# Weight-sum stores seven steps behind their load, thirteen pairs, and halves every eight steps, in a one-core attention and feed-forward block

## The chip, the core and the metric

The kernel runs on one core of a Trainium2 chip. A core has a matrix engine (TensorE, PE in the profile; its weight loads are PEld), a vector engine (VectorE, DVE), a scalar engine (ScalarE, ACT), GpSimd (POOL), and a queue engine, SyncE (SP), which issues nearly all transfers of this kernel to 16 DMA engines. Each engine works through its own instructions in order and waits for semaphores of the others. The metric is the device time of one execution in microseconds, as the median of several runs.

## What is computed

One layer with 256 tokens of 2048 features, in float32: three attention branches (six "forgetting" heads, six stick-breaking heads, four heads over a memory of 256 tokens), gated and merged, then a feed-forward part with a causal convolution over three tokens.

```python
h = rms_norm(x, g_mix[l])
proj = h @ w_in[l]
fq, fk, fv, f_logit, sq, sk, sv, mq, gates = jnp.split(proj, cuts, axis=-1)
...
g = jax.nn.sigmoid(gates.reshape(b, s, N_BRANCH, D_MODEL) + b_gate[l])
merged = (g[:, :, 0] * (o_fox @ w_br_fox[l])
          + g[:, :, 1] * (o_sb @ w_br_sb[l])
          + g[:, :, 2] * (o_mem @ w_br_mem[l]))
x = x + merged @ w_out[l]
h2 = rms_norm(x, g_ffn[l])
u = causal_depthwise_conv(h2 @ w_up[l], conv_w[l], conv_b[l])
u_gate, u_val = jnp.split(u, 2, axis=-1)
x = x + (jax.nn.silu(u_gate) * u_val) @ w_down[l]
```

## The kernel before

**Products.** Every weight is split into a high and a low part on the chip, and a product is the sum of three passes (high by high, low by high, high by low). `product` (L157) walks the 2048 rows of a weight in eight pieces of 256 rows by up to 512 columns. For each, `piece` (L136) loads the raw weights through SP's queue (L141) into one of four raw buffers, casts them to the high part on ACT (L142), and subtracts to get the low part on DVE (L143); four buffers hold high and low parts. Then twelve matmuls follow (two row tiles, two token tiles, three passes), and `tick` (L103) advances the generators by one step. So one step is one piece. Since there are four raw buffers, the load of a piece waits for the subtraction of the piece four steps before it.

**Stages.** In order: the memory's keys and values, then the heads' stages `mq`, `f0` to `f4`, `s0` to `s4` (products with parts of `w_in`; `f4` has 262 columns and `s4` 256, the others 512, and all have eight steps), with the work of the heads advanced by `tick` between the pieces. Then the gates and branches in two rounds (`m` = 0 and 1): gates by `product` for the first (`g0`) and by `blocked` for the others, then per round two times eight steps of branch products (forgetting three, memory two, stick-breaking three). After them the output product `o`, the up projection with the convolution, and the down projection `d`. `blocked` (L355) computes 2 by 2 blocks either with eight products ("e" in a plan) or with seven ("s"), which needs sums of weight blocks and of activations.

**Weight sums ahead.** The plans of `o` and `d` have 8 and 25 seven-product pairs. For each, three sums of blocks of the weights (`sums_in`, L247: instructions at L249, L250, L251 on DVE) are made ahead and kept in device memory. The list `halves` (L239) has two halves per pair. `pair_sums_ahead` (L282) takes a whole pair: a load of 1 MB (L292), the sums some steps later, a store of 1 MB (L302). `half_sums` (L259) takes half a pair: two loads of 256 KB (L268), sums of half the size, and a store of 512 KB (L278) from a single staging buffer, so that its next load waits until the store has landed. They are generators in `background`, and `tick` advances them one step per piece, except inside `blocked` for the gates, where `tick(beside=False)` leaves them alone.

- Heads' stages, from `f0` on (L771): pairs with period 6, sums after 3 steps, store after 5, in two staging buffers in turn, until `s3` has been issued (L938).
- Gates and branches (L962): halves with period 6, sums after 2, store after 4, until the output product begins (L1095). These stages have 48 such steps: 16 in the first gate's products and 16 in each round of branches.
- Up projection (L1132): the remaining 17 pairs, with period 8, sums after 1, store after 5.

**Order.** A planner orders the instructions of each engine from their dependences, program order and its own reckoning of durations. `in_order` (a name for `keep_in_program_order`, L234) pins an instruction behind the instruction traced just before it on the same engine; it says nothing of what comes after. The loads and stores of the sums, and the sums, are pinned in this way. The weight loads of the products in these stages are not pinned (`pinned[0]` is false from L732 on), so that the planner may draw them forward.

**Memory shared by tag.** The staging buffers of the pairs (`staged`, L764, tag "xres") share their place with `xs` (L951), sums of x that `x_sums` (L953) writes from its fifth step on, and later with the residual (`xres_again`, loaded again at L1067 in the second round of branches).

Of the kernel before, what the change touches and what calls it, by code (L numbers as in the profile page):

```python
# [9 lines left out]
F32 = mybir.dt.float32  # L10
# [5 lines left out]
P = 128  # L16
# [21 lines left out]
PF = 6  # L38
# [4 lines left out]
def hybrid_block(  # L43
# [25 lines left out]
    nc = tc.nc  # L69
# [31 lines left out]
    background = []  # L101
# [16 lines left out]
    issued = set()  # L118
# [84 lines left out]
    def k_tiles(name):  # L203
# [30 lines left out]
    in_order = tc.keep_in_program_order  # L234
# [4 lines left out]
    halves = deque(  # L239
        (name, by_k(w), nb, pr, h)  # L240
        for name, w, plans in (("o", w_out, o_plans), ("d", w_down, d_plans))
        for nb, plan in enumerate(plans)
        for pr in range(plan.count("s"))
        for h in range(2)
    )

    def sums_in(w):  # L247
        both = w[:, 1:2].to_broadcast([P, 2, w.shape[2]])
        in_order(nc.vector.tensor_tensor(w[:, 0:2], w[:, 0:4:3], both, ALU.add))  # L249
        in_order(nc.vector.tensor_tensor(w[:, T2], w[:, T1], w[:, T2], ALU.add))  # L250
        in_order(nc.vector.tensor_tensor(w[:, T4], w[:, T2], w[:, T4], ALU.add))  # L251

    def kept_for(name, nb, pr):
        if (name, nb, pr) not in sums_of:
            at = f"kept_{name}{nb}_{pr}"
            sums_of[name, nb, pr] = dram.tile([P, 4, 512], F32, tag=at, name=at)
        return sums_of[name, nb, pr]

    def half_sums(staging, period, add, store, end):  # L259

        while halves and end not in issued:
            name, wv, nb, pr, h = halves.popleft()
            kept = kept_for(name, nb, pr)
            w = staging(f"pre_{name}{nb}_{pr}_{h}").rearrange("p (i c) -> p i c", i=4)
            n0 = nb * PIECE + h * 256
            for n in range(2):
                in_order(
                    nc.sync.dma_start(  # L268
                        w.rearrange("p (k n) c -> p k n c", k=2)[:, :, n],
                        wv[:, 2 * pr : 2 * pr + 2, n0 + n * 512 : n0 + n * 512 + 256],  # L270
                    )
                )
            for _ in range(add):
                yield
            sums_in(w)
            for _ in range(store - add):
                yield
            in_order(nc.sync.dma_start(kept[:, :, h * 256 : (h + 1) * 256], w))  # L278
            for _ in range(period - store):
                yield  # L280

    def pair_sums_ahead(staging, period, add, store, end=None, delay=0):  # L282

        for _ in range(delay):
            yield
        while len(halves) > 1 and halves[0][-1] == 0 and end not in issued:
            name, wv, nb, pr, _ = halves.popleft()
            halves.popleft()
            kept = kept_for(name, nb, pr)
            w = staging(f"pre_{name}{nb}_{pr}")  # L290
            in_order(
                nc.sync.dma_start(  # L292
                    w.rearrange("p (k c) -> p k c", k=2), wv[:, 2 * pr : 2 * pr + 2, nb * PIECE : (nb + 1) * PIECE]
                )
            )
            w = w.rearrange("p (i c) -> p i c", i=4)
            for _ in range(add):
                yield
            sums_in(w)
            for _ in range(store - add):  # L300
                yield
            in_order(nc.sync.dma_start(kept, w))  # L302
            for _ in range(period - store):
                yield

    def parts(src, name):
        n = src.shape[1]
# [287 lines left out]
    gp = mix.enter_context(tc.tile_pool(name="gp", bufs=3))  # L595

    def block(name, dt=F32):
        return bp.tile([P, 1024], dt, tag="blk", name=name)

    def heads_of(b):  # L600
        return b.rearrange("p (h s) -> p h s", h=4)

    def rows_of(b):
        return b.rearrange("p (t n) -> p t n", t=NT)
# [68 lines left out]
    w = {}  # L673
# [30 lines left out]
    for k in range(KT):  # L704
# [18 lines left out]
        for _ in range(0 if k < 3 else 1 if k < 8 else 3):  # L723
            if squares:
                j, t = squares.popleft()
# [41 lines left out]
    def in_turn(name):  # L767
        turn[0] += 1
        return staged[:, turn[0] % 2]

    background.append(pair_sums_ahead(in_turn, PF, 3, 5, "s3"))  # L771
    qm = heads_of(block("qm"))
    y = norm_heads(ps, rstd, "mq")
    later(heads_T(y, qm, (gh[:, 2:3], gh[:, 2:3]), 2, "mq"))
# [160 lines left out]
        later(sb_head(h))  # L935

    ps = proj(C_SB + 1536, 512, "s3")
    issued.add("s3")  # L938
    vs[0] = rows_of(block("vs0"))
    for t in range(NT):  # L940
        nc.scalar.activation(vs[0][:, t], ps[t], AF.Copy, scale=rstd[:, t : t + 1])
# [11 lines left out]
    def x_sums():  # L953
# [6 lines left out]

    background.append(x_sums())
    background.append(  # L962
        half_sums(lambda name: gp.tile([P, 1024], F32, tag="pre", bufs=1, name=name), 6, 2, 4, "merged")
    )


# [143 lines left out]
    for nb, plan in enumerate(o_plans):  # L1110
# [19 lines left out]
    ends_tile = lambda name, dt: ff.tile([P, 2, PIECE], dt, tag="ends", bufs=1, name=name)  # L1130
    background.append(
        pair_sums_ahead(lambda name: ends_tile(name, F32).rearrange("p i c -> p (i c)"), 8, 1, 5, delay=DU)  # L1132
    )

# [196 lines left out]
```

## Time and profile before

| | |
|---|---|
| Median of 3 runs | 1465.25 us (1464.0 to 1466.06) |
| The profiled execution: its time, and its span | 1466.82 us, 1465.1 us |
| DMA, mean over the span | 260 GB/s, 381.08 MB |
| Pair loads and stores in the heads' stages | 12 and 12, 1 MB each |
| Half stores in gates and branches | 8, 512 KB each |
| Pair loads and stores in the up projection | 17 and 17, 1 MB each |

The span runs from the first to the last instruction that was profiled; the run's own time has a little more around it. A row of a timeline gives start and duration in microseconds, the engine (SPq is SP's queue), the line of the kernel, what is written from what, and in brackets how long the engine had been idle and what ended that. Rows of TensorE overlap, because matmuls are pipelined and their ends are modelled: the distance from start to start is what counts. A row of the view of a tile gives the line, the count, and shortest, median and longest duration in nanoseconds.

### The profile page before, as it was taken

The page shows a single profiled execution, that of the slowest core. Times are in us where ns is not written, and L with a number is a line of the kernel's source. Part 1 is how long each engine was busy: PE and PEld are TensorE (multiplying, and loading weights), DVE is VectorE, ACT ScalarE, POOL GpSimd, SP SyncE. Part 2 cuts the span into 40 slices and gives each one's busy share as a digit, 9 for nine tenths or more (in the row PEclk, how much of TensorE's full clock was granted, in tenths as well). Part 3 has the DMA queues.
Part 4 walks back from the last instruction along what each step waited for, and adds up shares of the span by engine and source line. Part 5 has one row for each costly group of instructions (what it writes and reads, how often), then busy time and mean ns, then how long its engine had stood idle before and what let it go on. Part 6 is the DMA issues. An engine that isn't in the chain of part 4 may idle for free.

```text
span 1465.1 us, 20555 instructions
## 1 busy us (share of the span) xinstructions
PE 1457.1 (99%) x7314; PEld 1231.1 (84%) x7314; DVE 1214.0 (83%) x1794; ACT 848.9 (58%) x1212; POOL 17.0 (1%) x48
## 2 busy tenths in 40 slices
PE   9999999999999999999999999999999999999998
PEld 7888888888888888878888888888888888888887
DVE  5778767776898899987987888888888877999878
ACT  6755445564654555545666656556556566676664
POOL 0000000110000000000000000000000000000000
PEclk9999999999999999999999999999999999999999
DMA  8697798677669676788878888888888866889995
GB/s 299 201 328 251 265 335 294 210 230 211 215 203 284 193 228 198 257 269 265 269 218 231 273 276 300 276 283 291 282 282 293 273 202 203 251 289 323 309 327 216
DMA packets 164262, 381.08 MB, mean 260 GB/s; under 512 B 12298, under 2 KB 29598, under 8 KB 160190
## 3 DMA queue, kind: packets, MB, share of 16 engines
q1 hardware_dynamic: 162750, 377.52, 78.9%
q10 hardware_dynamic: 1328, 2.11, 0.4%
q8 instruction: 57, 0.93, 0.3%
q14 instruction: 47, 0.39, 0.1%
q0 software_dynamic: 80, 0.13, 0.0%
HBM read 343.01 MB, written 36.70 MB: 259 GB/s over the span
## 4 chain that ended last, share of the span: by engine, by line
PE 95%; DVE 2%; DMA 2%; issue 1%; ACT 0%; SPq 0%; DVEq 0%; ACTq 0%
PE u L1220 22%; PE u L1221 11%; PE xg L318 4%; PE xg L317 4%; PE xg L316 4%; PE xd L317 3%; PE xd L316 3%; PE xd L318 3%; PE f L316 2%; PE f L317 2%; PE f L318 2%; PE s L318 2%; PE s L316 2%; PE s L317 2%; PE yd L317 2%; PE yd L316 2%
## 5 line engine op out<-in xcount | busy, mean ns | idle before, releaser
L1220 PE MATMUL u<-hT,hi_u 128*128 128x512 f32 x1232 | 428.3, 394 | 0.0
L1221 PE MATMUL u<-hT,lo_u 128*128 128x256 f32 x1232 | 341.3, 277 | 0.0
L1220 PEld LDWEIGHTS u<-hT,hi_u 128*128 128x128 f32 x1232 | 231.0, 188 | 53.6
L143 DVE TENSOR_TENSOR lo_u<-raw_u,hi_u 128x1024 fp32r<-128x1024 f32 x176 | 215.3, 1224 | 73.2 <-ACT hi_u L142 72.7
L142 ACT CAST hi_u<-raw_u 128x1024 fp32r<-128x1024 f32 x176 | 184.7, 1050 | 136.7 <-PE u L1220 106.4
L1221 PEld LDWEIGHTS u<-hT,lo_u 128*128 128x128 f32 x1232 | 231.3, 188 | 0.0
L311 DVE TENSOR_TENSOR lo_d<-raw_d,hi_d 128x1024 fp32r<-128x1024 f32 x88 | 106.7, 1222 | 17.2 <-ACT hi_d L310 14.9
L310 ACT CAST hi_d<-raw_d 128x1024 fp32r<-128x1024 f32 x88 | 91.7, 1053 | 39.4 <-PE xd L317 11.6
L310 ACT CAST hi_g<-raw_g 128x1024 fp32r<-128x1024 f32 (+1 forms) x80 | 77.1, 972 | 48.9 <-PE xg L317 18.6
L311 DVE TENSOR_TENSOR lo_g<-raw_g,hi_g 128x1024 fp32r<-128x1024 f32 (+1 forms) x80 | 88.7, 1120 | 4.2 <-ACT hi_g L310 4.1
L142 ACT CAST hi_f<-raw_f 128x1024 fp32r<-128x1024 f32 (+1 forms) x40 | 38.6, 967 | 51.6 <-PE f L317 46.3
L316 PE MATMUL xg<-hi_g,xT 128*128 128x512 f32 x175 | 68.1, 389 | 0.0
L318 PE MATMUL xg<-lo_g,xT 128*128 128x512 f32 x175 | 68.1, 389 | 0.0
L317 PE MATMUL xg<-hi_g,xT 128*128 128x512 f32 x175 | 68.1, 389 | 0.0
L143 DVE TENSOR_TENSOR lo_f<-raw_f,hi_f 128x1024 fp32r<-128x1024 f32 (+1 forms) x40 | 44.6, 1118 | 21.9 <-ACT hi_f L142 21.2
L1220 PE MATMUL u<-hT_rest,hi_u 128*128 128x512 f32 x176 | 62.0, 394 | 0.0
L142 ACT CAST hi_b<-raw_b 128x1024 fp32r<-128x1024 f32 x32 | 33.5, 1051 | 47.7 <-DMA raw_b<-in_w_br_fox_dram 13.5
L143 DVE TENSOR_TENSOR lo_s<-raw_s,hi_s 128x1024 fp32r<-128x1024 f32 (+1 forms) x40 | 44.5, 1114 | 19.9 <-ACT hi_s L142 19.5
L142 ACT CAST hi_s<-raw_s 128x1024 fp32r<-128x1024 f32 (+1 forms) x40 | 38.2, 961 | 36.9 <-PE s L317 21.5
L1171 ACT ACTIVATE y<-u,taps 128x256 f32<-128x256 f32 x88 | 49.6, 596 | 15.6 <-DVE u L1166 15.5
L318 PE MATMUL xd<-lo_d,aT 128*128 128x512 f32 x148 | 57.6, 389 | 0.0
L316 PE MATMUL xd<-hi_d,aT 128*128 128x512 f32 x148 | 57.6, 389 | 0.0
(520 smaller groups left out, 3475.9 us busy)
## 6 DMA issues: line engine op xcount, KB each, us to landing
raw_u<-in_w_up_dram SPq DMA_DIRECT2D x176, 512.0 KB, 4.8
raw_g<-in_w_in_dram SPq DMA_DIRECT2D x96, 512.0 KB, 4.5
raw_d<-in_w_down_dram SPq DMA_DIRECT2D x63, 512.0 KB, 5.6
pre_d<-in_w_down_dram SPq DMA_DIRECT2D x17, 1024.0 KB, 7.3
kept_d<-pre_d SPq DMA_DIRECT2D x17, 1024.0 KB, 6.2
raw_f<-in_w_in_dram SPq DMA_DIRECT2D x32, 512.0 KB, 4.7
raw_s<-in_w_in_dram SPq DMA_DIRECT2D x32, 512.0 KB, 4.9
raw_t_d<-kept_d SPq DMA_DIRECT2D x25, 512.0 KB, 6.1
```

What stands on the lines that cost most here:

```text
L142: pin(nc.scalar.copy(hi[:, :m], raw[:, :m]))
L143: pin(nc.vector.tensor_tensor(lo[:, :m], raw[:, :m], hi[:, :m].bitcast(F32), ALU.subtract))
L310: nc.scalar.copy(hi[:, :n], src)
L311: nc.vector.tensor_tensor(lo[:, :n], src, hi[:, :n].bitcast(F32), ALU.subtract)
L316: fix(nc.tensor.matmul(o, lhsT=ah, rhs=w[0], start=first, stop=False))
L317: fix(nc.tensor.matmul(o, lhsT=al, rhs=w[0], start=False, stop=False))
L318: fix(nc.tensor.matmul(o, lhsT=ah, rhs=w[1], start=False, stop=last))
L1171: nc.scalar.activation(y, u[:, 2:], AF.Identity, scale=tap(2), bias=tap(3))
L1220: nc.tensor.matmul(ps[i], lhsT=hi[:, j, c], rhs=hT(k + j), start=first, stop=False)
L1221: nc.tensor.matmul(ps[i][:, :S], lhsT=lo[:, j, c], rhs=hT(k + j)[:, :S], start=False, stop=last)
```

## The change

In the heads' stages the store of a pair is made seven steps after its load in place of five, which is one step after the next pair's load. To allow this, the generator keeps the stores that are due in a list with the step at which each is to go. The generator ends after thirteen pairs, not when `s3` has been issued: the thirteenth pair is loaded in the first step of `s4` and stored in its last. In gates and branches a half takes eight steps, not six, and its store goes after five, not four, so that six halves are made there in place of eight. The up projection's 17 pairs keep their steps.

```diff
-    def pair_sums_ahead(staging, period, add, store, end=None, delay=0):
-
+    def pair_sums_ahead(staging, period, add, store, most=99, delay=0):
+
+        due = deque()
+        clock = 0
         for _ in range(delay):
             yield
-        while len(halves) > 1 and halves[0][-1] == 0 and end not in issued:
+
+        def step():
+            while due and due[0][0] <= clock:
+                _, kept, w = due.popleft()
+                in_order(nc.sync.dma_start(kept, w))
+
+        while len(halves) > 1 and halves[0][-1] == 0 and most:
+            most -= 1
             name, wv, nb, pr, _ = halves.popleft()
             halves.popleft()
             kept = kept_for(name, nb, pr)
...
             w = w.rearrange("p (i c) -> p i c", i=4)
-            for _ in range(add):
+            due.append((clock + store, kept, w))
+            for t in range(period):
+                if t == add:
+                    sums_in(w)
+                step()
+                clock += 1
                 yield
-            sums_in(w)
-            for _ in range(store - add):
-                yield
-            in_order(nc.sync.dma_start(kept, w))
-            for _ in range(period - store):
-                yield
+        while due:
+            step()
+            clock += 1
+            yield
...
-    background.append(pair_sums_ahead(in_turn, PF, 3, 5, "s3"))
+    background.append(pair_sums_ahead(in_turn, PF, 3, 7, most=13))
...
-    issued.add("s3")
...
-        half_sums(lambda name: gp.tile([P, 1024], F32, tag="pre", bufs=1, name=name), 6, 2, 4, "merged")
+        half_sums(lambda name: gp.tile([P, 1024], F32, tag="pre", bufs=1, name=name), 8, 2, 5, "merged")
```

## Prediction

> **What bounds the kernel now.** I read the first two parts of the page first.
>
> ```profile
> span 1465.1 us, 20555 instructions
> PE 1457.1 (99%) x7314; PEld 1231.1 (84%) x7314; DVE 1214.0 (83%) x1794; ACT 848.9 (58%) x1212; POOL 17.0 (1%) x48
> ```
>
> TensorE is busy for all but 8.0 us (1465.1 - 1457.1). The change touches no matmul, so it can win only moments in which a matmul starts late. I therefore went through TensorE's timeline start by start. In a 512-column product the starts are 0.23 us apart (the first two rows below); what exceeds that is lost. Outside the start-up there are three losses near 1 us, one in the heads' stages and two in the second round of branches:
>
> ```profile
> 201.60 0.39 PE L317 MATMUL s<-hi_s,xT 128*128 128x512 f32 x1
> 201.83 0.39 PE L318 MATMUL s<-lo_s,xT 128*128 128x512 f32 x1
> 202.33 0.50 PE L316 MATMUL s<-hi_s,xT 128*128 128x512 f32 x1
> 202.67 0.40 PE L317 MATMUL s<-hi_s,xT 128*128 128x512 f32 x1
> 203.59 0.50 PE L318 MATMUL s<-lo_s,xT 128*128 128x512 f32 x1 [0.53 <-DVE lo_s L143]
> 203.93 0.40 PE L316 MATMUL s<-hi_s,xT 128*128 128x512 f32 x1
> ...
> 636.59 0.39 PE L317 MATMUL b<-hi_b,oT 128*128 128x512 f32 x1
> 637.70 0.50 PE L318 MATMUL b<-lo_b,oT 128*128 128x512 f32 x1 [0.72 <-DVE lo_b L143]
> ...
> 660.35 0.39 PE L317 MATMUL b<-hi_b,oT 128*128 128x512 f32 x1
> 661.48 0.50 PE L318 MATMUL b<-lo_b,oT 128*128 128x512 f32 x1 [0.74 <-DVE lo_b L143]
> ```
>
> - At 201.8: steps of 0.50, 0.34, 0.92 and 0.34 in place of 0.23 each, so 0.27 + 0.11 + 0.69 + 0.11 = **1.18 us**.
> - At 636.6: 1.11, so 0.88, and the stretched step behind it, taken from the first group, 0.11: **0.99 us**.
> - At 660.4: 1.13, so 0.90 + 0.11 = **1.01 us**.
>
> Together 3.18 us, 0.22% of the time. That is about all the change can win; what remains is whether it wins it, and what it makes late elsewhere.
>
> **Part 1: the store goes seven steps behind its load.** The chain of waits around 201 says what was late:
>
> ```profile
> 192.38 0.69 DVE staged L251
> ...
> 193.52 7.68 DMA raw_s<-in_w_in_dram
> ...
> 201.23 1.06 ACT hi_s L142
> ```
>
> The last of the sums (L251) ends at 193.07. The store (L302 in the next group) waited for it and is issued at 193.09; only then comes the weight load behind it on SP's queue, at 193.52, which takes 7.68 us. Its cast and subtraction come too late for TensorE. That load's buffer had been free since 189.5, when the subtraction four pieces back (the four raw buffers) ended, and the sums come directly behind that subtraction:
>
> ```profile
> 188.76 0.70 DVE L143 TENSOR_TENSOR lo_f<-raw_f,hi_f 128x524 fp32r<-128x524 f32 x1 [0.76 <-ACT hi_f L142]
> ```
>
> and on SP's queue:
>
> ```profile
> 193.09 0.34 SPq L302 DMA_DIRECT2D kept_o<-staged  x1
> ...
> 205.41 0.42 SPq L292 DMA_DIRECT2D staged<-in_w_down_dram  x1
> 206.23 0.37 SPq L141 DMA_DIRECT2D raw_s<-in_w_in_dram  x1
> 210.93 0.34 SPq L302 DMA_DIRECT2D kept_o<-staged  x1
> ```
>
> So the weight load lost 193.52 - 189.5 = 4.0 us behind a store that could not go yet. With the store written two ticks later it is pinned behind the weight piece of that tick, so this load must go ahead of it. It then lands 4.0 us earlier, at about 197.2; cast (1.06) and subtraction (1.24) end by 199.6, ahead of the 202.3 at which TensorE wants it. The next load stays behind the store, but is wanted one piece (12 x 0.23 = 2.7 us) later. Gain: 1.18 us. The other stores gain nothing: there the planner already issues the next pair's load and a weight piece ahead of the store, as the rows at 205 to 211 show (load, weight piece, store), because the store is pinned only behind what was traced before it and the later load is not pinned behind the store. The staging buffer that the store holds longer is reused 12 ticks after its load, so five ticks (five pieces, 13 us) remain for a landing of 6.6 us (quoted below): no wait.
>
> **Part 2: the thirteenth pair.** Its load, three sums and store now fall into the narrow stage of 256 columns, where a piece lasts half as long. The sums, from the views of the two staging tiles:
>
> ```profile
> L249 DVE TENSOR_TENSOR staged<-staged x12: 1205/1218/1221, 84.9 to 281.3; 128x1024 f32<-128x1024 f32 x12
> DMA to landing us min/median/max: 4.2/6.6/7.7
> ```
>
> ```profile
> L249 DVE TENSOR_TENSOR pre_d<-pre_d x8: 684/685/685, 314.9 to 648.0; 128x512 f32<-128x512 f32 x8
> L251 DVE TENSOR_TENSOR pre_d<-pre_d x8: 418/423/425, 317.1 to 652.7; 128x256 f32<-128x256 f32 x8
> ```
>
> A pair costs DVE 1.22 + 2 x 0.69 = 2.60 us (L251 from the chain above; L250 is as large), a half 0.685 + 2 x 0.42 = 1.53 us. In all, DVE trades two halves (3.06) for a pair (2.60): 0.46 us less, of no worth by itself under a full TensorE. The bytes are the same. What counts is where they fall (timelines of ACT, DVE and TensorE, then the page's list of DMA issues):
>
> ```profile
> 301.51 0.61 ACT L142 CAST hi_s<-raw_s 128x512 fp32r<-128x512 f32 x1
> ```
>
> ```profile
> 304.96 0.69 DVE L143 TENSOR_TENSOR lo_s<-raw_s,hi_s 128x512 fp32r<-128x512 f32 x1 [1.10 <-ACT hi_s L142]
> 307.22 1.29 DVE L143 TENSOR_TENSOR lo_s<-raw_s,hi_s 128x512 fp32r<-128x512 f32 x2 [1.10 <-ACT hi_s L142]
> 309.59 1.23 DVE L143 TENSOR_TENSOR lo_g<-raw_g,hi_g 128x1024 fp32r<-128x1024 f32 x1 [1.07 <-PE s L317]
> ```
>
> ```profile
> 306.91 0.28 PE L318 MATMUL s<-lo_s,xT 128*128 128x256 f32 x1
> 312.90 0.39 PE L318 MATMUL g<-lo_g,xT 128*128 128x512 f32 x1
> ```
>
> ```profile
> raw_s<-in_w_in_dram SPq DMA_DIRECT2D x32, 512.0 KB, 4.9
> ```
>
> DVE idles 1.10 + 1.10 + 1.07 = 3.27 us in these few steps, which covers the 2.60 us of sums; without that cover they would stand in front of the stage's last subtractions. The store is pinned behind the stage's last weight piece, and the first gate piece competes with it. A weight load just behind such a store took 7.68 us against a median of 4.9, so 2.8 us more. The first gate piece is split by 310.82 (309.59 + 1.23) and wanted at 312.90: 2.08 us of slack. Store ahead of it on the queue: 2.8 - 2.08 = 0.7 us late, plus 0.1 of stretched pitch, 0.8. Store behind it: 0. Below nothing is excluded, since nothing is late in that stage now. If sums and store both delayed it and the idle time covered nothing, 2.60 + 2.8 - 2.08 = 3.3 us, the outer end. The quoted queue rows have the store now before, now after the weight piece whose buffer comes free just after the sums, so I take the middle of 0 and 0.8: **0.4 us lost**.
>
> How fast that queue drains decides the 0.7:
>
> ```profile
> 193.00:202.00 9.00, 9.00 (x45) 7.43 (x43) 2.86 (x6) 3.20 (x7) 0.00 (x0) 1.00 1.03 398
> ```
>
> (Last columns: DMA busy share and GB/s.) With the DMA engines full, at 193 to 202, 398 GB/s went through. The Trainium skill (DMA: Bandwidth & Descriptors, section Where 436 GB/s comes from) puts the limit between HBM and SBUF at about 358 GB/s per core; the row is above it, and the measurement decides. By the page a 1.05 MB store would hold the queue 2.9 us, by the row 2.6 us; the sum would be 0.3 us worse by the page.
>
> **Part 3: gates and branches, eight ticks per half.** Only the first gate projections and the two rounds of branches advance this generator, 16 ticks each. Period 6 starts eight halves in 48 ticks and lets one straddle from the first round into the second; period 8 starts six, two per stretch. In the second round that means two sets of sums and two stores in place of three. And a second wait shrinks. There is one staging buffer, so a load waits for the store before it to land (SP's waits from 430 to 670, total, times and longest; then SP's timeline):
>
> ```profile
> SPq L268 <- DMA kept_d<-pre_d: 11.9, 5, 4.7
> ```
>
> ```profile
> 615.18 0.53 SPq L278 DMA_DIRECT2D kept_d<-pre_d  x1
> 615.76 0.62 SPq L1067 DMA_DIRECT2D xres_again<-in_x_dram  x1
> 621.13 0.88 SPq L268 DMA_DIRECT2D pre_d<-in_w_down_dram  x2
> 622.11 1.44 SPq L141 DMA_DIRECT2D raw_b<-in_w_br_sb_dram  x3
> 636.20 0.52 SPq L278 DMA_DIRECT2D kept_d<-pre_d  x1
> 640.34 0.88 SPq L268 DMA_DIRECT2D pre_d<-in_w_down_dram  x2
> ```
>
> The next branch's weights (L141, 622.11) stand behind such a load, which stood behind the store: 5.9 us from store to load here, 4.1 us at 636.20 to 640.34, then 512 KB more on the full queue. Now the second round's loads come behind its first and ninth piece, early in each half, not ahead of the stick-breaking branch's weights. The stall at 636.6 loses one set of sums (1.53 us, more than its 0.99) from DVE's queue ahead of the late subtraction, and that at 660.4 loses another and the load at 640.34. The set that stays falls behind the third piece of each half, where nothing is late now. Gain: 2.00 us if both go, 0 if neither. I take both: 2.00.
>
> **The sum.** 1.18 + 2.00 - 0.4 = 2.78 us. The profiled execution took 1466.82 us around its span of 1465.1; the sum makes that 1464.04. The median of the runs shown is 1.57 lower, 1465.25, and becomes **1462.5**.
>
> **Rivals.**
> - *The x loads make the branch stalls.* The two 1 MB reloads of x (the row at 615.76 is one) fall into the same 25 us; if they alone make the weights late, sums and stores matter little. For it: the weights behind them were late by DMA. Against: the stall at 660 comes some 40 us after that row. Then 1465.25 - 1.18 + 0.4 = 1464.5.
> - *The change does not do what it says in the heads' stages*: the planner had most stores there already, and reorders around the one that counts so that another weight piece is late. Then 1465.25 - 2.00 + 0.4 = 1463.7.
> - *Slower: ACT waits for the thirteenth store.* The weight sums of x (xs, cast at L332) take the staging buffers' memory, so their first cast waits until the last store has landed. The planner draws them forward into the narrow stage:
>
> ```profile
> 293.27 0.61 ACT L332 CAST xs<-xr 128x512 fp32r<-128x512 f32 x1
> ```
>
>   Now the last store cannot be issued before about 304.1: its sums, 2.60 us, stand behind the fourth subtraction of the narrow stage, which I put beside the fifth cast at 301.51. It lands 6.6 us later at 310.7, and the xs cast ends at 311.3. Casts of weight pieces queued behind it on ACT wait too: for the fifth piece (now cast at 301.51), cast 0.61 and subtraction 0.69 would end at 312.6, wanted at 306.9: 5.7 us, so 1465.25 - 3.18 + 5.7 = 1467.8. It decides for slower where the cast stands ahead of the sixth piece or an earlier one: a piece lasts about 1.4 us there (four lie between the rows at 306.91 and 312.90), so the sixth costs 4.3, above the 3.18 won. Against: if the planner reckons with the later store, it places the cast later, and it is needed only in the gate stages.
>
> **How the numbers follow.** Forecast 0.50, x loads 0.17, heads unchanged 0.15, ACT's wait 0.13, anything else 0.05. Differences within 0.2% (2.9 us) cannot be told from none. The forecast's own range, residue 0 to 0.8 and the runs' scatter of 1 us, is 1461.3 to 1463.5; about half of it lies below 1462.3, and with what I may have missed (smaller late starts elsewhere) faster gets 0.34. The x loads, unchanged heads and the rest of the forecast are "same": 0.56. ACT's wait from its dearer places makes slower 0.10. The range reaches from 1461.3 to 1466.5, up to but not over the dear end of the slower rival.
>
> **What would show it.** Right: no late start of TensorE near 201, 636 and 660; near 190 a weight load ahead of the store that went at 193.09; SP's waits at L268 for kept_d well under 11.9 us; at most 0.8 us lost where the gates begin. Wrong: late starts in the last 256-column stage, ACT idle ahead of the xs cast, or branch subtractions as late as now with fewer sums ahead of them.

## The result and the profile after

| | before | changed |
|---|---|---|
| Median of 14 runs | 1464.72 us | 1462.28 us |
| Ratio, with its 95% interval | | 0.9982 [0.9974, 0.9991] |
| Profiled execution, its span | 1465.1 us | 1459.8 us |

The change makes the kernel 2.44 us faster; 1462.5 us was forecast, 2.75 below the 1465.25 shown then. The first lines of the changed kernel's page:

```profile
span 1459.8 us, 20547 instructions
PE 1454.0 (100%) x7314; PEld 1230.1 (84%) x7314; DVE 1213.4 (83%) x1791; ACT 850.0 (58%) x1212; POOL 19.3 (1%) x48
```

The idle time of TensorE went from 8.0 to 5.8 us (1459.8 - 1454.0). The two spans differ by more than the medians. Part of it lies ahead of `f0` in code that the change doesn't reach (the first matmul of s0 starts 1.54 us earlier, in the rows below). So I compare stretches between matmuls. TensorE's timeline, before and then after: the first matmul of s0, of the gates, of the first branches and of the output product.

```profile
193.86 0.40 PE L316 MATMUL s<-hi_s,xT 128*128 128x512 f32 x1
...
312.43 0.40 PE L316 MATMUL g<-hi_g,xT 128*128 128x512 f32 x1
...
446.78 0.39 PE L316 MATMUL b<-hi_b,oT 128*128 128x512 f32 x1
...
663.89 0.39 PE L316 MATMUL xo<-hi_o,mT 128*128 128x512 f32 x1
```

```profile
192.32 0.40 PE L328 MATMUL s<-hi_s,xT 128*128 128x512 f32 x1
...
309.68 0.40 PE L328 MATMUL g<-hi_g,xT 128*128 128x512 f32 x1
...
444.39 0.39 PE L328 MATMUL b<-hi_b,oT 128*128 128x512 f32 x1
...
658.84 0.39 PE L328 MATMUL xo<-hi_o,mT 128*128 128x512 f32 x1
```

From s0 to the gates it is 118.57 before and 117.36 after (1.21 won), through the first round's gates 134.35 and 134.71 (0.36 lost), from there to the output product 217.11 and 214.45 (2.66 won). From there to the last matmul both take 796.7. The place of the late start near 200 is now regular, 0.23 from start to start:

```profile
200.74 0.39 PE L329 MATMUL s<-hi_s,xT 128*128 128x512 f32 x1
200.97 0.39 PE L330 MATMUL s<-lo_s,xT 128*128 128x512 f32 x1
201.20 0.39 PE L328 MATMUL s<-hi_s,xT 128*128 128x512 f32 x1
```

SP's queue shows why. One weight load now stands between the pair's load and the store, and the store still waits for its sums, with one weight load fewer behind it:

```profile
186.95 0.42 SPq L301 DMA_DIRECT2D staged<-in_w_out_dram  x1
188.06 0.37 SPq L141 DMA_DIRECT2D raw_s<-in_w_in_dram  x1
191.66 0.34 SPq L292 DMA_DIRECT2D kept_o<-staged  x1
192.09 10.48 SPq L141 DMA_DIRECT2D raw_s<-in_w_in_dram  x5
```

Over both rounds a load of a half (L268) still waits for the store before it, but once, not five times (SP's waits from 430 to 670: total, times, longest). In the second round SP issues the loads of two halves and two stores, in place of two and three:

```profile
SPq L268 <- DMA kept_d<-pre_d: 3.6, 1, 3.6
```

```profile
602.62 0.97 SPq L268 DMA_DIRECT2D pre_d<-in_w_down_dram  x2
...
619.32 0.53 SPq L278 DMA_DIRECT2D kept_d<-pre_d  x1
...
623.65 0.97 SPq L268 DMA_DIRECT2D pre_d<-in_w_down_dram  x2
...
641.09 0.53 SPq L278 DMA_DIRECT2D kept_d<-pre_d  x1
```

The one late start over 0.2 us left after `f0` is not in the profile of before. It lies in the gates, where no background step runs; here are TensorE's timeline and then DVE's:

```profile
421.76 0.39 PE L329 MATMUL xg<-hi_t_g,xT 128*128 128x512 f32 x1
422.28 0.50 PE L330 MATMUL xg<-lo_t_g,xT 128*128 128x512 f32 x1
422.62 0.40 PE L328 MATMUL yg<-hi_t_g,xs 128*128 128x512 f32 x1
```

```profile
420.39 0.69 DVE L440 TENSOR_TENSOR t_g<-raw_g 128x512 f32<-128x512 f32 x1 [1.69 <-DMA raw_g<-in_w_in_dram]
421.00 1.22 DVE L323 TENSOR_TENSOR lo_t_g<-t_g,hi_t_g 128x1024 fp32r<-128x1024 f32 x1
```

DVE waits 1.69 us for a weight transfer that an addition of the next pair needs (L440), and the subtraction that TensorE needs (L323) stands behind it: 0.29 + 0.11 = 0.40 us.

### The profile page after: what moved, and what is told of

Its sections match the earlier page's. It is cut to its first block, busy times and chain, and to the rows that moved or that the text cites. A ratio compares the mean times of both kernels' runs of the same rounds, so it can differ in the third digit from the quotient of the medians.

```text
span 1459.8 us, 20547 instructions
## 1 busy us (share of the span) xinstructions
PE 1454.0 (100%) x7314; PEld 1230.1 (84%) x7314; DVE 1213.4 (83%) x1791; ACT 850.0 (58%) x1212; POOL 19.3 (1%) x48
## 4 chain that ended last, share of the span: by engine, by line
PE 97%; DVE 1%; DMA 1%; issue 0%; SPq 0%; ACT 0%; DVEq 0%; ACTq 0%
PE u L1231 22%; PE u L1232 11%; PE xd L329 3%; PE xd L330 3%; PE xd L328 3%; PE xg L330 3%; PE xg L329 3%; PE xg L328 3%; PE s L328 2%; PE s L330 2%; PE f L330 2%; PE f L328 2%; PE f L329 2%; PE s L329 2%; PE b L330 2%; PE b L328 2%
## 5 line engine op out<-in xcount | busy, mean ns | idle before, releaser
L323 DVE TENSOR_TENSOR lo_d<-raw_d,hi_d 128x1024 fp32r<-128x1024 f32 x88 | 106.7, 1222 | 16.2 <-ACT hi_d L322 13.8
L323 DVE TENSOR_TENSOR lo_g<-raw_g,hi_g 128x1024 fp32r<-128x1024 f32 (+1 forms) x80 | 88.6, 1119 | 4.1 <-ACT hi_g L322 4.1
```

Of the source, the lines that this page charges most:

```text
L323: nc.vector.tensor_tensor(lo[:, :n], src, hi[:, :n].bitcast(F32), ALU.subtract)
```

## The experiments

Each run has a profile, and all are read in the same way: the three stretches as above, and the late starts over 0.2 us with the stretched step behind each. Times are in us; the ratio is to the kernel before on the same chip.

| kernel | s0 to gates | first gates | to the output product | late starts (place: size) | median | ratio |
|---|---|---|---|---|---|---|
| before | 118.57 | 134.35 | 217.11 | 202: 1.2, 594: 0.5, 637: 1.0, 660: 1.0 | 1464.72 | |
| before, again | 118.19 | 134.42 | 216.38 | 201: 0.8, 628: 1.0, 635: 1.0 | 1464.1 (one run) | |
| changed | 117.36 | 134.71 | 214.45 | 422: 0.4 | 1462.28 | 0.9982 [0.9974, 0.9991] |
| changed, again | 117.35 | 134.62 | 214.92 | 422: 0.3, 592: 0.6 | 1461.94 | 0.9984 [0.9974, 0.9993] |
| lag only | 117.35 | 134.83 | 217.13 | 382: 0.5, 630: 0.8, 636: 0.9, 660: 0.9 | 1463.46 | 0.9995 [0.9986, 1.0004] |
| halves only | 117.92 | 134.69 | 214.31 | 201: 0.5, 381: 0.4 | 1462.85 | 0.9989 [0.9981, 0.9998] |
| store after five | 118.37 | 134.68 | 214.77 | 201: 0.9, 381: 0.2 | 1462.68 | 0.9988 [0.9979, 0.9997] |
| halves of six | 117.35 | 134.87 | 216.15 | 381: 0.6, 629: 0.7, 635: 0.9 | 1463.54 | 0.9994 [0.9985, 1.0003] |
| twelve pairs | 117.35 | 134.25 | 214.54 | none | 1462.64 | 0.9989 [0.9979, 1.0] |
| halves four later | 117.35 | 134.27 | 216.58 | 594: 0.3, 622: 0.2, 659: 1.3 | 1463.46 | 0.9995 [0.9982, 1.0007] |
| x later (on before) | 117.84 | 134.64 | 215.78 | 201: 0.5, 381: 0.3, 593: 0.3, 635: 1.1 | 1463.19 | 0.9991 [0.9982, 1.0] |
| additions pinned | 117.35 | 134.25 | 214.31 | none | 1461.14 | 0.9978 [0.9967, 0.9988] |
| additions pinned, again | 117.35 | 134.25 | 214.31 | none | 1461.14 | 0.9978 [0.9969, 0.9987] |

Intervals of the times are about 2.5 us wide, so the stretches tell more than the medians: where nothing is late they repeat to 0.01 us.

**Are the late starts a property of the kernels?** The kernel before once more:

> The kernel before, a second profiled execution. Theory (the late starts follow from the order of the instructions): late starts again near 200, 636 and 660, 2.5 to 3.5 us in all. Rival (they are accidents of one execution): at least two of the three are absent.

and the changed one:

> The changed kernel, a second profiled execution and more times. Theory: no late start near 200, 636 and 660; one of 0.2 to 0.6 us somewhere in the gates; ratio to before 0.998. Rival (accidents of one execution): a late start of over 0.5 us at one of the three places.

Near 200 and 636 they came again; the one at 660 did not, and one of the same size stood at 628, in the first of the three pieces of the stick-breaking branch whose third piece is late near 636. In all it is 2.8 us, as expected. TensorE's timeline of that second execution of before:

```profile
200.61 0.40 PE L317 MATMUL s<-hi_s,xT 128*128 128x512 f32 x1
201.53 0.50 PE L318 MATMUL s<-lo_s,xT 128*128 128x512 f32 x1 [0.53 <-DVE lo_s L143]
...
628.67 0.40 PE L317 MATMUL b<-hi_b,oT 128*128 128x512 f32 x1
629.59 0.50 PE L318 MATMUL b<-lo_b,oT 128*128 128x512 f32 x1 [0.52 <-DVE lo_b L143]
```

So the sum in the second branches came again (2.0 us both times), the single places did not. The changed kernel had none of them again. In the gates it was late near 422 again, by 0.3 us, and by 0.6 near 592, where the kernel before had lost 0.5 in its first profile.

**The lag alone.**

```diff
-pair_sums_ahead(in_turn, PF, 3, 7, most=13)
+pair_sums_ahead(in_turn, PF, 3, 7, most=12)
...
-half_sums(..., 8, 2, 5, "merged")
+half_sums(..., 6, 2, 4, "merged")
```

> Twelve pairs in the heads' stages as before, their stores seven steps behind the load; halves as before (period 6, sums after 2, store after 4). Theory (the store ahead of a weight load makes the late start near 201): the load goes ahead of the store and that late start of 1.18 us is gone, those of about 1 us near 636 and 660 stay: 1.2 us faster than before, ratio near 0.9992. Rival (the heads' late start is the planner's order as a whole, not this store): a late start of about 1 us stays in s0, time as before, ratio 1.0000.

The heads' stretch is 117.35, all that the change wins there, and the branches keep 2.6 us of late starts. The theory holds. The time, 0.9995, has the expected 0.9992 in its interval, and 1.0000 too.

**The lag undone.**

```diff
-pair_sums_ahead(in_turn, PF, 3, 7, most=13)
+pair_sums_ahead(in_turn, PF, 3, 5, most=13)
```

> The changed kernel with the stores of the pairs five steps behind their load again (thirteen pairs, halves with eight steps). Theory: the weight load behind the store near 192 goes late again and the late start near 200 is back with 1.0 to 1.3 us: 1.2 us slower than the changed kernel, ratio to before near 0.9990. Rival (the thirteenth pair or the halves won it): no late start near 200, time as the changed kernel, ratio 0.9982.

The weight load is behind the store again (SP's queue, then TensorE):

```profile
187.00 0.42 SPq L301 DMA_DIRECT2D staged<-in_w_out_dram  x1
191.60 0.34 SPq L292 DMA_DIRECT2D kept_o<-staged  x1
192.03 1.36 SPq L141 DMA_DIRECT2D raw_s<-in_w_in_dram  x2
```

```profile
200.99 0.40 PE L329 MATMUL s<-hi_s,xT 128*128 128x512 f32 x1
201.91 0.50 PE L330 MATMUL s<-lo_s,xT 128*128 128x512 f32 x1 [0.53 <-DVE lo_s L143]
```

0.9 us are back, a little under the expected 1.0 to 1.3. That one store makes the heads' late start is thereby shown from both sides. Its size varies: in the five profiles with that store five steps behind its load the heads' stretch is 0.5 to 1.2 us above 117.35, and in all eight with seven steps it is 117.35.

**The halves alone, and undone.** Alone, on the changed kernel's text, with 18 pairs left to the up projection:

```diff
-DU = 22
+DU = 14
...
-pair_sums_ahead(in_turn, PF, 3, 7, most=13)
+pair_sums_ahead(in_turn, PF, 3, 5, most=12)
```

> Twelve pairs, their stores five steps behind the load as before; halves with eight steps, sums after 2, store after 5. One pair more (18) is left to the up projection, which starts eight steps earlier with them. Theory (sums and waiting loads of the halves make the branches' late starts): those near 636 and 660 are gone, 2.0 us, and the one near 201 stays at 1.2 us: 2.0 us faster than before, ratio near 0.9986. Rival (the two reloads of x make them): both stay, each 0.8 to 1.0 us, ratio 1.0000.

Undone:

```diff
-half_sums(..., 8, 2, 5, "merged")
+half_sums(..., 6, 2, 4, "merged")
```

> The changed kernel with halves of six steps again (sums after 2, store after 4), so eight halves; one pair fewer (16) is left to the up projection. Theory: the late starts in the second round of branches are back with 1.5 to 2.2 us in all: 2.0 us slower than the changed kernel, ratio to before near 0.9996. Rival (the x reloads, or chance, decide these): they stay away, ratio 0.9982.

With eight steps both late starts of the second branches are gone; with six, 1.6 us are back. So the halves' rhythm decides. The late start near 201 stayed, but with 0.5 us, not the expected 1.2. The first run alone does not exclude the reloads of x, because the rhythm moves one of them on the queue. Before, the second reload stands behind a store that waits for its sums (615.18 and 615.76 in the prediction's rows), 1.4 us ahead of the first matmul of these branches at 617.14. With eight steps no store stands there and both reloads go together, here in the changed kernel, 4.7 us ahead of that matmul at 614.34:

```profile
609.67 1.22 SPq L1078 DMA_DIRECT2D xres_again<-in_x_dram  x2
```

**Place or number.**

```diff
+    def four_later(gen):
+        for _ in range(4):
+            yield
+        yield from gen
...
-        half_sums(lambda name: gp.tile([P, 1024], F32, tag="pre", bufs=1, name=name), 8, 2, 5, "merged")
+        four_later(half_sums(lambda name: gp.tile([P, 1024], F32, tag="pre", bufs=1, name=name), 8, 2, 5, "merged"))
```

> The changed kernel with the halves' generator begun four steps later: as many sums and stores and the same eight steps, but in the second round of branches the loads then stand ahead of the stick-breaking weights and the sums behind the seventh and fifteenth piece, where those of before stood. Theory (it is the place of the loads and sums, more than their number): late starts near 636 and 660 come back with 1 to 2 us. Rival (the number of sums and stores decides): they stay away.

Half of each. Only 1.3 us near 660 came back, nothing near 636, although the load stands ahead of the stick-breaking weights again. DVE's timeline near 660, then TensorE's:

```profile
652.87 0.68 DVE L249 TENSOR_TENSOR pre_d<-pre_d 128x512 f32<-128x512 f32 x1
653.58 0.42 DVE L250 TENSOR_TENSOR pre_d<-pre_d 128x256 f32<-128x256 f32 x1
654.04 0.43 DVE L251 TENSOR_TENSOR pre_d<-pre_d 128x256 f32<-128x256 f32 x1
...
658.72 1.22 DVE L143 TENSOR_TENSOR lo_b<-raw_b,hi_b 128x1024 fp32r<-128x1024 f32 x1
```

```profile
658.58 0.39 PE L329 MATMUL b<-hi_b,oT 128*128 128x512 f32 x1
660.00 0.50 PE L330 MATMUL b<-lo_b,oT 128*128 128x512 f32 x1 [1.02 <-DVE lo_b L143]
```

DVE has no gap from 650 to 660, and 1.5 us of sums stand ahead of the round's last subtraction, for which TensorE is 1.3 us late. As the number of halves is that of the changed kernel, it is their place that matters here. But sums ahead of that subtraction are not enough: the kernel before, in its second profile, has them there too, and nothing is late near 660 (DVE's timeline, the first sum and the last subtraction):

```profile
646.11 0.68 DVE L249 TENSOR_TENSOR pre_d<-pre_d 128x512 f32<-128x512 f32 x1
...
656.59 1.21 DVE L143 TENSOR_TENSOR lo_b<-raw_b,hi_b 128x1024 fp32r<-128x1024 f32 x1
```

Near 636 the sums stand ahead of the third stick-breaking subtraction in this run as well, and it is on time. What differs is DVE's idle time ahead of the first one. Before, the sums begin at 633.01, and DVE had waited 2.96 us for the cast of that branch's first piece:

```profile
629.97 2.53 DVE L143 TENSOR_TENSOR lo_b<-raw_b,hi_b 128x1024 fp32r<-128x1024 f32 x2 [2.96 <-ACT hi_b L142]
...
636.42 1.22 DVE L143 TENSOR_TENSOR lo_b<-raw_b,hi_b 128x1024 fp32r<-128x1024 f32 x1
```

With halves four later DVE has other work there and does not wait:

```profile
628.12 1.22 DVE L143 TENSOR_TENSOR lo_b<-raw_b,hi_b 128x1024 fp32r<-128x1024 f32 x1
...
631.59 0.69 DVE L249 TENSOR_TENSOR pre_d<-pre_d 128x512 f32<-128x512 f32 x1
...
634.66 1.23 DVE L143 TENSOR_TENSOR lo_b<-raw_b,hi_b 128x1024 fp32r<-128x1024 f32 x1
```

All five profiles with halves of six steps have this wait, with 2.96 to 3.84 us, and the late start near 636. So the late start near 636 goes with a wait and sums together; no run took one of the two away alone.

**The reloads of x.**

```diff
-                if (m, n, i) == (1, 0, 1):
+                if (m, n, i) == (1, 1, 2):
                     xres = cst.tile([P, NT, D], F32, tag="xres", name="xres_again")
                     for t in range(NT):
-                        nc.sync.dma_start(xres[:, t], xv[:, t])
+                        in_order(nc.sync.dma_start(xres[:, t], xv[:, t]))
```

> The kernel before, with the two reloads of x held back behind the last branch weights. Theory (sums and waiting loads of the halves alone are enough): the late starts near 636 and 660 stay with 1.5 to 2.1 us. Rival (the halves hurt only together with the x reloads): both go, and the kernel is about 2 us faster than before if the reloads cost nothing in their new place, where they compete with the output product's weights.

With the reloads behind the last branch weights, before still loses 1.1 us near 635, less than the expected 1.5 to 2.1, and nothing near 660. So the halves alone are enough for the late start near 636. About the second one this single profile says little: the kernel before itself had none near 660 in its second profile, and 1.0 us at 628 instead.

**The thirteenth pair.**

```diff
-DU = 22
+DU = 14
...
-pair_sums_ahead(in_turn, PF, 3, 7, most=13)
+pair_sums_ahead(in_turn, PF, 3, 7, most=12)
```

> The changed kernel with twelve pairs in the heads' stages, not thirteen (stores seven steps behind, halves with eight steps); one pair more (18) is left to the up projection, which starts eight steps earlier with them. Theory (the thirteenth pair costs nothing, since DVE and the queue have room in the last 256-column stage): from the first matmul of s0 to the first of the gates 117.35 us as in the changed kernel, time as the changed kernel, ratio 0.9982. Rival (the 0.4 us that the prediction charged for it): 0.4 us shorter to the middle of the first gates, ratio 0.9979.

With twelve pairs the heads' stretch is 117.35, with thirteen the same: the pair costs nothing there. The first gates are 0.46 us shorter than in the changed kernel, as the rival expects, but that is the late start at 422, and the next run has the same 134.25 with thirteen pairs. The times (0.9989, expected 0.9982 or 0.9979) cannot tell.

**The late start left in the gates.**

```diff
-            nc.vector.tensor_tensor(u[:, 0], b0[:, 0], b0[:, 1], ALU.add)
-            nc.vector.tensor_tensor(u[:, 1], b0[:, 1], b1[:, 1], ALU.add)
+            in_order(nc.vector.tensor_tensor(u[:, 0], b0[:, 0], b0[:, 1], ALU.add))
+            in_order(nc.vector.tensor_tensor(u[:, 1], b0[:, 1], b1[:, 1], ALU.add))
```

> The changed kernel with the first two of the four additions that prepare a seven-product pair of the gates pinned in program order on DVE. Theory (the late start left in the gates, 0.40 us at 421.8, comes from such an addition that the planner put ahead of a subtraction and that waits for its weight transfer): no late start above 0.1 us remains in the gates, 0.4 us off the changed kernel, ratio to before near 0.9979. Rival (the transfer itself is late for the subtraction's own work, or the pinned additions come too late): a late start of 0.3 us or more stays in the gates.

> The changed kernel with the first two additions of a gates' pair pinned, a second time. Theory: again no late start above 0.15 us from f0 to the output product, and 0.4 us below the changed kernel of the same chip, though times alone may not tell 0.4 us. Rival (its first profile was lucky): a late start of 0.3 us or more in the gates.

In both executions nothing over 0.1 us is late from `f0` to the output product: 134.25 and 214.31, the shortest of all. The subtractions now go ahead of the addition (DVE's timeline of the first execution, the same kind of place):

```profile
378.04 1.22 DVE L323 TENSOR_TENSOR lo_t_g<-t_g,hi_t_g 128x1024 fp32r<-128x1024 f32 x1 [0.66 <-ACT hi_t_g L322]
379.19 2.35 DVE L323 TENSOR_TENSOR lo_g<-raw_g,hi_g 128x1024 fp32r<-128x1024 f32 x2
381.46 0.69 DVE L440 TENSOR_TENSOR t_g<-raw_g 128x512 f32<-128x512 f32 x1
```

Its 1461.14 us is the lowest median of all kernels here. Against before, the interval of its ratio lies wholly below 1. Against the changed kernel the 0.8 to 1.1 us in the medians are within the scatter, and the 0.6 and 1.0 us by the three stretches rest on two profiles each. Twelve pairs had nothing over 0.2 us late in the gates without the pins, so one such profile alone would prove little.

## Why the prediction was right

- **What bounds it.** Right: all that was won are late starts of TensorE. Their sum, 3.18 us, was nearly the ceiling; it left out a late start of 0.5 us near 594. The additions-pinned kernel, without any of them, is 3.6 us under before (1464.7 to 1461.14), against 3.18 + 0.5 = 3.7.
- **Part 1, 1.18 us.** Right in mechanism: the weight load goes ahead of the store, and lag alone and lag undone show that this is the cause. In size it was at the upper end: 1.21 us by these two profiles, 0.8 by the second one of before, 0.5 in two other kernels with the old lag. The other stores gained nothing, as said.
- **Part 2, 0.4 us lost.** The term was mis-sized: it measured 0. The first gate piece's load went ahead of the store, so the wait behind the store fell on the second piece, which had room. ACT's timeline shows both, and also the wait of the slower rival:

```profile
305.48 1.05 ACT L142 CAST hi_g<-raw_g 128x1024 fp32r<-128x1024 f32 x1 [0.82 <-PE s L329]
307.24 0.62 ACT L344 CAST xs<-xr 128x512 fp32r<-128x512 f32 x1 [0.71 <-DMA kept_d<-staged]
310.17 1.05 ACT L142 CAST hi_g<-raw_g 128x1024 fp32r<-128x1024 f32 x1 [2.31 <-DMA raw_g<-in_w_in_dram]
```

  ACT does wait 0.71 us for the thirteenth store, but the planner placed that cast behind the first gate piece's, so no weight cast of the narrow stage stood behind it. The rival's mechanism is real, its place was not there.
- **Part 3, 2.00 us.** Right in size: 2.0 us of late starts in the second branches in both profiles of before (1.6 and 2.6 in two other kernels with six-step halves), none in the changed kernel. That the halves' rhythm makes them is shown by the run with it alone and the run with it undone. The reason given was half right. Sums do stand ahead of the late subtractions, but with halves four later they stand ahead of the one near 636 too, and the load ahead of the stick-breaking weights, and nothing is late there. What the profiles with that late start share, and this run lacks, is DVE's idle wait of 3.0 to 3.8 us for the branch's first cast. The reloads of x, a rival, are not needed for the late start near 636; whether they take part in the other one stays open.
- **What the sum left out.** Late starts in the gates, 0.1 to 0.6 us in either kernel, which move from place to place. They were seen as "smaller late starts elsewhere" and given no term. No run shows that the change makes or cures them.
- **The sum.** 2.78 us forecast, 2.44 and, in the later set of runs, 2.80 measured (1464.74 to 1461.94). That it fits so closely is in part luck. By the three stretches the first pair of profiles gives 3.5 us and the second 2.1, because Part 1 and the late starts in the gates vary by some tenths each, and the 0.4 us charged for Part 2 made up for such losses.

## What to carry to other kernels

A store that waits for a computation holds up every load behind it on the same queue: here a weight load went at 193.52, 4.0 us after its buffer was free. Give the store a longer lag, so that by its turn the loads which could go have gone. Two steps between sums and store were too few for one of these stores, four were enough for all; that four is also the number of load buffers may be chance, as no other lag was tried for the pairs. When an engine is 99% busy, list its late starts one by one, the small ones too: their sum is about the ceiling of a change in order, and each names its own cause. And an addition that waits for a transfer should not stand ahead of work that is ready and that the busiest engine waits for.

## What was not expected of the hardware

The DMA engines moved more than the prediction's 398 GB/s in the same place of the changed kernel (windows; the last columns are DMA share and GB/s):

```profile
192.00:201.00 9.00, 9.00 (x43) 7.49 (x43) 3.70 (x7) 4.49 (x8) 0.00 (x0) 1.00 1.03 407
```

And in the profiled execution of twelve pairs (1471.12 us, where its other runs lie between 1461.43 and 1463.84) the up projection took 498.1 us from its first to its last matmul, in place of 489.8 in the changed kernel, at the same granted clock of 1.00. In its middle 568 matmuls started in 100 us in place of 579. One window of this execution, then the same of the changed kernel:

```profile
950.00:1050.00 100.00, 100.00 (x568) 86.77 (x567) 85.59 (x140) 59.47 (x93) 0.00 (x0) 1.00 0.85 282
```

```profile
950.00:1050.00 100.00, 100.00 (x579) 87.37 (x578) 85.66 (x137) 57.95 (x88) 0.00 (x0) 1.00 0.86 283
```

What slowed it stays open. DVE, ACT and the DMA engines had no more to do: in the three windows from 850 to 1150 DVE and ACT did 407 and 265 instructions in place of 421 and 273, and the DMA engines moved 274 to 282 GB/s in place of 283 to 288. One execution of halves four later took 1471.88 us, but it left no profile.
